# Rotations ahead of the value casts, and layer 0's last adds on VectorE with layer 1's tables and first weights in place early

## The chip, the cores and the metric

The kernel runs on one core of a Trainium2 chip. The metric is the device time of one execution in microseconds, median of three runs. The core has a matrix engine (TensorE, in the profile PE for its matmuls and PEld for the loading of stationary operands), a vector engine (VectorE, DVE), an activation engine (ScalarE, ACT), a general engine (GpSimd, POOL) and a queue from which most DMAs are issued (SyncE, SP). Each engine executes its instructions in the order in which they stand in its queue; between engines there are semaphores.

## The reference

A block of two layers for a diffusion model: 512 latent tokens and 256 context tokens, width 1024. Layer 0 has windowed attention with grouped keys and a sink, layer 1 differential attention with 8 heads. Each is followed by an MLP with squared ReLU. Cut to what matters:

```python
for i in range(DEPTH):                                # 2 layers
    mod_x = silu(c) @ w_ada[i] + b_ada[i]             # six vectors; mod_c likewise
    hx, hc = x * (1 + sc1) + sh1, ctx * (1 + csc1) + csh1
    ax, ac = mixer_i(hx, hc)                          # q, k rotated (x only), v not
    x  = layer_norm(alpha * x + g1 * ax)
    fx = square(relu((x * (1 + sc2) + sh2) @ w1)) @ w2
    x  = layer_norm(alpha * x + g2 * fx)              # ctx likewise in layer 0
```

In `mixer_i` the projections are `q = rope(hx @ wq)`, `k = rope(hx @ wk)`, `v = hx @ wv`. The rotation multiplies each half of a head by tables of cosines and sines. Everything is in 32 bits.

## The kernel before, in words

The 768 tokens are six blocks of 128 (`tb` 0 to 3 latent, 4 and 5 context). Every product is done three times at reduced width: an operand is split into a high part (a cast on ACT) and a low part (a subtraction on DVE), and `mm3` (L323 to L327) multiplies high by high, high by low and low by high into one PSUM bank. So each weight goes through `wsplit` (L300): a DMA into a raw buffer, ACT's cast `h`, DVE's subtraction `l`. The helper `split` does the same to activations.

The order of TensorE's instructions is written out by the kernel itself: `Flow` is a planner that runs jobs (Python generators) against estimated engine times and emits TensorE's work in the order in which its plan has the operands ready. Only TensorE's order is fixed in this way (`manual_schedule`); the order on DVE, ACT, POOL and SP is chosen by the framework when the kernel is built, within the data dependencies and the order of the program text, unless the kernel adds an order edge (`ORDER`). PSUM is divided into two double banks (`sS`, tiles of 1024) and four single banks (`sm_`, tiles of 512). A bank is given back by `give` when the planner sees its reader done; for the chip the wait is a semaphore.

Three places are touched.

*Start of layer 0.* `start_load` loads, for each quarter `g` of the width, two blocks of modulation weights, two slices of the tokens and one query weight `Wq[0]`. `start_x` modulates the tokens: for each slice ACT writes the high part, DVE the value and (for latent tokens) the low part, POOL the low part of the context tokens. `kv_job` and `proj` multiply. `kv_post` takes the keys and values of one block from PSUM: ACT copies the values to `vv`, DVE rotates the keys (three products, POOL adds them), and `split` makes the stacked operand that TensorE transposes into `kT`.

*End of layer 0.* `mlp_pipe` ends in `last_y`: the last products of the second MLP matrix. By then `fx` holds most of the MLP's output, and POOL folds it into `acc`, gated, in 24 operations (`fold`). The remaining products stay in PSUM. `final` multiplies each by the gate on DVE (`g_tmp`, in scratch buffers of tag `tmp`, of which there are three, shared with the normalised tiles `hx_v`) and adds the product to `acc`: on DVE where `last` is true, else on POOL. The statistics follow, then `normalise` and, in `ln_job`, transposes and the split operands `hx` of layer 1. In the second half (`half == 1`) only block 5 is added on DVE:

```python
r = gated_add(R.pool, lambda x: sm_.give(slot, x), acc[tb], half, pt, p, gates[0 if tb < NXB else 1],
              half == 1 if l else half == 0 or tb == ntb - 1)
```

*Start of layer 1.* `pre1` loads the weights of head 0 (four parts `u`) and multiplies blocks 0 to 3 while layer 0 ends. The rest happens once the pool of layer 0 is closed: the tables `cosT` and `sinT` are loaded, `proj1` multiplies blocks 4 and 5 and then the other heads, and `post1` takes each block from PSUM: first the values (`split` into `vt`), then the rotation of queries and keys, then `split` into `sk` and `sq`, which TensorE transposes to `kT_ps` and `qT_ps`. `scores1` needs all six blocks of a head.

## Time and profile before

| | |
|---|---|
| median of 3 runs | 1653.91 us (1649.16 to 1657.4) |
| profiled execution | 1652.57 us, of which the span from the first to the last instruction is 1650.8 |
| mean granted TensorE clock | 0.989 |
| TensorE busy | 1576.2 us (95%) |
| DVE / ACT / POOL busy | 1141.4 / 794.2 / 452.0 us |
| DMA | 181.18 MB, 110 GB/s on average |

Times in the profile are microseconds from the start of the span. A row of a timeline has the start, the duration, the engine, the line, the operation, out<-in, the shape and the count; in brackets stand the idle time of the engine just before it and what ended it. A row of waits has who waited for whom, the total, the number of times and the longest. Where a helper records an operation, the line is that of the helper (L260 DVE, L264 ACT, L268 POOL, L275 DMA, L314 the low part of a weight), and the tile names tell the place.

### The profile page before, as it was taken

The numbers are of one execution on the slowest core, as the hardware profiler recorded it, in microseconds if no ns is written. First come the engines' busy times: TensorE is split into PE (matmuls) and PEld (weight loads), VectorE is DVE, ScalarE is ACT, GpSimd is POOL, SyncE is SP. The second block draws the span as 40 slices with busy tenths as digits, with TensorE's granted clock in tenths as the row PEclk, the third lists the DMA queues.
The fourth block names the chain that finished last, engine by engine and source line by source line (L and its number), as shares of the span: only waits on it lengthen the run. The fifth ranks groups of instructions, "written<-read, shape, count | busy, mean of one in ns | idle before, by whom it ended". The sixth has DMA issues, their size and how long they took to land.

```text
span 1650.8 us, 25195 instructions
## 1 busy us (share of the span) xinstructions
PE 1576.2 (95%) x9465; PEld 1380.7 (84%) x9465; DVE 1141.4 (69%) x2201; ACT 794.2 (48%) x1683; POOL 452.0 (27%) x369
## 2 busy tenths in 40 slices
PE   7899999999999999999997999999989799999998
PEld 5788777789888888889986999899877788888896
DVE  4655676688786768877556777777665886565667
ACT  3465676375343343334416555555552745444550
POOL 1343544106111211221191222220100023233363
PEclk9999999999999999999998999999999999999999
DMA  9110550533344444444423122211122233333321
GB/s 373 43 52 20 192 179 27 187 132 123 101 156 156 146 131 130 163 130 153 153 68 115 49 74 64 75 46 39 49 95 110 93 118 109 103 102 102 99 74 59
DMA packets 66435, 181.18 MB, mean 110 GB/s; under 512 B 7368, under 2 KB 13320, under 8 KB 66312
## 3 DMA queue, kind: packets, MB, share of 16 engines
q1 hardware_dynamic: 66312, 179.56, 32.5%
q8 instruction: 74, 1.21, 0.3%
q14 instruction: 49, 0.40, 0.1%
HBM read 168.49 MB, written 11.04 MB: 109 GB/s over the span
## 4 chain that ended last, share of the span: by engine, by line
PE 69%; DVE 11%; ACT 6%; issue 5%; POOL 5%; DMA 4%; SPq 0%; DVEq 0%; POOLq 0%; ACTq 0%
PE y_ps L325 8%; PE y_ps L326 8%; PE y_ps L327 8%; PE h_ps L325 7%; PE h_ps L326 7%; PE h_ps L327 7%; PE qkv_ps L325 2%; PE qkv_ps L326 2%; PE qkv_ps L327 2%; PE o_ps L1379 2%; PE pT_ps L1397 2%; PE s_ps L1758 2%; POOL acc L268 1%; PE o_ps L1796 1%; DVE w_l L314 1%
## 5 line engine op out<-in xcount | busy, mean ns | idle before, releaser
L325 PE MATMUL y_ps<-w_h,hid 128*128 128x512 f32 (+1 forms) x648 | 255.4, 394 | 1.1 <-DVE fx L260 1.1
L326 PE MATMUL y_ps<-w_l,hid 128*128 128x512 f32 (+1 forms) x648 | 254.6, 393 | 0.9 <-DVE w_l L314 0.9
L327 PE MATMUL y_ps<-w_h,hid 128*128 128x512 f32 (+1 forms) x648 | 254.7, 393 | 0.0
L314 DVE TENSOR_TENSOR w_l<-w_raw,w_h 128x1024 fp32r<-128x1024 f32 (+1 forms) x133 | 160.8, 1219 | 58.9 <-ACT w_h L264 56.8
L264 ACT CAST w_h<-w_raw 128x1024 fp32r<-128x1024 f32 (+1 forms) x133 | 131.7, 1001 | 108.1 <-PE y_ps L327 76.4
L268 POOL TENSOR_TENSOR w_sum<-w_raw 128x512 f32<-128x512 f32 x26 | 59.1, 2274 | 329.0 <-DMA w_raw<-in_w 264.8
L260 DVE TENSOR_TENSOR w_half<-w_raw,w_half 128x512 fp32r<-128x512 f32 x130 | 107.8, 840 | 56.7 <-ACT w_half L264 56.2
L327 PEld LDWEIGHTS y_ps<-w_h,hid 128*128 128x128 f32 x648 | 122.0, 188 | 28.6
L326 PEld LDWEIGHTS y_ps<-w_l,hid 128*128 128x128 f32 x648 | 122.1, 188 | 26.4 <-DVE w_l L314 1.8
L325 PEld LDWEIGHTS y_ps<-w_h,hid 128*128 128x128 f32 x648 | 122.1, 188 | 25.9 <-DVE fx L260 1.5
L264 ACT CAST w_half<-w_raw 128x512 fp32r<-128x512 f32 x130 | 79.1, 621 | 131.8 <-PE h_ps L327 97.1
L325 PE MATMUL qkv_ps<-w_h,hx 128*128 128x384 f32 (+1 forms) x384 | 128.1, 334 | 3.0 <-ACT w_h L264 2.9
L326 PE MATMUL qkv_ps<-w_l,hx 128*128 128x384 f32 (+1 forms) x384 | 123.5, 322 | 1.7 <-DVE w_l L314 1.7
L327 PE MATMUL qkv_ps<-w_h,hx 128*128 128x384 f32 (+1 forms) x384 | 123.2, 321 | 0.0
L268 POOL TENSOR_TENSOR e<-e,sm 128x512 f32<-128x512 f32 (+2 forms) x96 | 92.7, 978 | 109.1 <-DVE sm L260 84.0
L264 ACT ACTIVATE relu<-relu 128x384 f32<-128x384 f32 (+3 forms) x104 | 69.3, 671 | 60.6 <-DVE relu L260 59.4
L260 DVE TENSOR_TENSOR fx<-y_ps,fx 128x512 f32<-128x512 f32 x110 | 75.2, 685 | 33.4 <-PE y_ps L327 33.0
L268 POOL TENSOR_TENSOR rope<-rope,rope 128x256 f32<-128x256 f32 (+1 forms) x40 | 33.9, 847 | 222.7 <-DVE rope L260 175.9
L268 POOL TENSOR_TENSOR w_raw<-w_raw,w_sum 128x512 f32<-128x512 f32 x26 | 39.2, 1508 | 178.3 <-DVE w_half L260 140.7
L673 DVE CUSTOM_DVE_ANT_0 w_raw<-w_raw,cB 128x512 f32<-128x512 f32 x112 | 84.1, 785 | 3.7 <-PE y_ps L327 3.2
L264 ACT ACTIVATE e<-e,nm 128x513 f32<-128x513 f32 (+2 forms) x96 | 65.9, 687 | 32.4 <-DVE nm L260 25.7
L325 PEld LDWEIGHTS qkv_ps<-w_h,hx 128*128 128x128 f32 x384 | 73.0, 190 | 4.8 <-ACT w_h L264 3.3
(268 smaller groups left out, 4323.9 us busy)
## 6 DMA issues: line engine op xcount, KB each, us to landing
w_raw<-in_w SPq DMA_DIRECT2D x128, 512.0 KB, 3.6
w_raw<-in_w_adaT SPq DMA_DIRECT2D x56, 512.0 KB, 3.8
w_raw<-in_w_ada SPq DMA_DIRECT2D x24, 512.0 KB, 3.8
w_raw<-in_b_w SPq DMA_DIRECT2D x32, 384.0 KB, 3.6
raw<-in_w_ada SPq DMA_DIRECT2D x16, 512.0 KB, 9.6
w_raw<-in_a_wq SPq DMA_DIRECT2D x8, 512.0 KB, 7.9
w_raw<-in_a_wo SPq DMA_DIRECT2D x8, 512.0 KB, 4.5
w_raw<-in_b_wo SPq DMA_DIRECT2D x8, 512.0 KB, 4.4
```

What stands on the lines that cost most here:

```text
L260: fn(**kw)
L264: fn(**kw)
L268: fn(**kw)
L314: last["split"] = nc.vector.tensor_tensor(**kw)
L325: nc.tensor.matmul(out=o, lhsT=lh, rhs=rh, start=start, stop=False, **kw)
L326: nc.tensor.matmul(out=o, lhsT=lh, rhs=rl, start=False, stop=False, **kw)
L327: last["pe"] = nc.tensor.matmul(out=o, lhsT=ll, rhs=rh, start=False, stop=stop, **kw)
L673: i = fn(**kw)
L1379: nc.tensor.matmul(out=po[odd * HD:odd * HD + HD, 0:256], lhsT=vv[:, kb, kvh], rhs=pt_[:, odd * 256:odd * 256 + 256], start=(i == 0), stop ...
L1397: nc.tensor.transpose(out=pp[:, c * P:(c + 1) * P], in_=es[j][:, i * P:(i + 1) * P], identity=ident)
L1758: nc.tensor.matmul(out=sp[:, c * 512:c * 512 + 384], lhsT=qTt[:, tt, hl, qb * P:(qb + 1) * P], rhs=kS[:, tt, c * 384:c * 384 + 384], start ...
L1796: nc.tensor.matmul(out=po[:, qp * 256:(qp + 1) * 256], lhsT=vt[:, kb, vl], rhs=pt_[:, pl, a * 256:a * 256 + 256], start=(kp == 0 and pl == ...
```

## The change

It has two parts. The first is in the order of the program text. In `kv_post` and `post1` the rotations, and for context blocks the key split, are stated ahead of the values' casts. In layer 0 the values of four blocks, and then of two, are copied by one instruction (`v_copy`). At the start of layer 0 the cast and the split of the last query weight get an order edge behind the last modulation of the tokens.

The second is at the border of the layers. All adds of `final` in layer 0 go to DVE. `fx` moves to a pool of its own on the right side of the memory, which is closed after the folds (`folded`), and a pool `early1` takes its place: it holds layer 1's tables, rotation scratch, `vt`, `sk`, `sq` and the residual tiles. In `pre1` the first two of head 0's four weights get buffers of their own (the MLP's `relu` and raw buffers), and all six blocks are multiplied there, the context blocks in single banks. The special latency that the planner assumed for the last block's normalisation (2.5) is dropped in favour of the common one (6.0).

```diff
@@ wsplit
-        a = ac(n, [q, hg], nc.scalar.copy, out=h[:, :n], in_=raw[:, :n])
+        last["cast"] = nc.scalar.copy(out=h[:, :n], in_=raw[:, :n])
+        a = fl.op("A", act(n), [q, hg])
@@ last_y, final
-                              half == 1 if l else half == 0 or tb == ntb - 1)
+                              half == 1 or l == 0)
...
                 for tb in range(ntb):
                     fold(half, tb, None)
+            R.folded()
@@ start_load
             Wq[0].append(wsplit(t["a_wq"][0, g]))
+            last["q"] = last["cast"], last["split"]
@@ start_x (ia: the last ACT modulation, id_: the last DVE low part)
+            if g == 3:
+                for w, x in zip(last["q"], (ia, id_)):
+                    tc.add_manual_dep(w.ins, x.ins.name, ORDER, reason="queue order")
@@ kv_post
+        def v_copy(tb, n, src, p):
+            return ac(n * P, [p], nc.scalar.copy, out=vv[:, tb:tb + n],
+                      in_=src.rearrange("p (b s g d) -> p b s g d", s=2, g=2, d=HD)[:, :, 1])
...
-            e = ac(P, [p], nc.scalar.copy, out=vv[:, tb], in_=vv_)
             if tb < NXB:
                 kr, e, r = rope(pool, kk_, tb, 2, p, ...)
                 if tb == NXB - 1:
-                    sS.give(kvslots[0], e)
+                    sS.give(kvslots[0], v_copy(0, NXB, kvS, e))
...
             if tb == NTB - 1:
-                sm_.give(kvslots[1], r)
+                sm_.give(kvslots[1], v_copy(NXB, NTB - NXB, kvm, r))
@@ layer 0's MLP
+    right = ExitStack()
+    fxpool = right.enter_context(tc.tile_pool(name="fx0", bufs=1, side="right", reuse_waits="tile"))
...
+            def folded(self):
+                right.close()
+                st2["ep"] = right.enter_context(tc.tile_pool(name="early1", bufs=1, side="right", reuse_waits="tile"))
...
-            fl.add(ln_job(pool, acc[tb], tb, st2["hx"], st2["A"], st2["B"], ready2, st, r, None,
-                          LNLAT if tb < NTB - 1 else 2.5), 0)
+            fl.add(ln_job(pool, acc[tb], tb, st2["hx"], st2["A"], st2["B"], ready2, st, r), 0)
@@ pre1
-            st2["W"] = [wsplit(t["b_w"][0, u], 768) for u in range(4)]
+            own = [pool.tile([P, n], F32R, name="w_" + x, tag=tag, bufs=2) for n, tag in ((TOK, "xr"), (1024, "raw"))
+                   for x in "hl"]
+            st2["W"] = W = [wsplit(t["b_w"][0, u], 768, hl=own[2 * u:2 * u + 2] + [None, None] if u < 2 else None)
+                            for u in range(4)]
...
+            for tb in range(NTB):
+                j = tb % 2
+                if tb >= NXB:
+                    yield sm_.ok
+                    pj, give = psm("qkv_ps"), (lambda x, i=sm_.take(): sm_.give(i, x))
+                else:
...
+                for u in range(4):
+                    yield W[u].t
+                    p = qkv_mm(W, st2["hx"], tb, pj, u)
+                    if tb == NTB - 1:
+                        fl.finish(W[u].rel)
+                st2["pre"][tb] = pj, p, give
@@ attn1 (cosT, sinT, rope, vt, sk, sq, rs_* now from ep = st2["ep"])
-        lamv = pool.tile([P, 4, HD], F32, name="lamv", tag="rope", bufs=2)
+        lamv = pool.tile([P, 4, HD], F32, name="lamv", tag="oraw", bufs=3)
@@ post1
-            _, e = split(P, p, pt[:, 256:384], vt[:, tb, 0], vt[:, tb, 1])
             if isx:
-                qk, e2, r = rope(pool, pt[:, 0:256].rearrange("p (g d) -> p g d", d=HD), tb, 4, p)
+                qk, e2, r = rope(ep, pt[:, 0:256].rearrange("p (g d) -> p g d", d=HD), tb, 4, p)
                 kr = qk[:, 2:4]
-                give([e, e2])
...
+            def v_split(d):
+                return split(P, d, pt[:, 256:384], vt[:, tb, 0], vt[:, tb, 1])[1]
+            if isx:
+                give(v_split(e2))
...
-                give([e, d1])
+                give(v_split(d1))
```

## The prediction

> **What bounds the kernel now.** The page comes first: which engine fills the span, and what clock it was granted.

> ```profile
> span 1650.8 us, 25195 instructions
> PE 1576.2 (95%) x9465; PEld 1380.7 (84%) x9465; DVE 1141.4 (69%) x2201; ACT 794.2 (48%) x1683; POOL 452.0 (27%) x369
> PEclk9999999999999999999998999999999999999999
> ```

> TensorE is busy for 1576.2 of 1650.8 us, and neither its 9465 matmuls nor their shapes are touched by the change. So the change can win only from the 74.6 us in which TensorE stands still, and from stretches at a lower granted clock (the 8 in PEclk, 22nd of the 40 slices, 867 to 908 us, is one). Those 74.6 us come next, from the view of TensorE's own waits; its columns are total us, times, longest. These are the rows that the edits can reach.

> ```profile
> PE kT_ps L1662 <- DVE sk L260: 7.8, 6, 2.3
> PE xn_t L550 <- DVE g_tmp L584: 5.4, 3, 2.8
> PE qkv_ps L325 <- ACT w_h L264: 2.9, 1, 2.9
> PE xn_t L550 <- POOL rstd L268: 1.8, 1, 1.8
> PE qkv_ps L326 <- DVE w_l L314: 1.7, 2, 1.2
> PE q_ps L325 <- DVE rope L260: 1.5, 1, 1.5
> PE xn_t L550 <- ACT hx_v L264: 0.9, 1, 0.9
> PE kv_ps L327 <- POOL hx L268: 0.7, 1, 0.7
> ```

> Then I place them with the view of stages: start and end, width, busy PE, PEld, DVE, ACT, POOL, then the granted clock.

> ```profile
> 50.00:66.00 16.00, 13.83 (x85) 11.81 (x83) 11.65 (x31) 7.42 (x19) 5.78 (x7) 1.00 0.13 37
> 848.00:863.00 15.00, 15.00 (x66) 12.06 (x65) 6.75 (x7) 1.06 (x1) 15.00 (x11) 1.00 0.18 54
> 863.00:892.50 29.50, 18.59 (x98) 14.22 (x96) 21.30 (x44) 17.19 (x50) 8.87 (x11) 0.95 0.18 71
> 888.50:900.00 11.50, 7.06 (x26) 6.28 (x27) 9.02 (x18) 10.68 (x28) 0.55 (x1) 0.55 0.32 103
> 1168.00:1180.00 12.00, 9.68 (x40) 8.01 (x39) 8.55 (x13) 5.44 (x12) 0.00 (x0) 0.72 0.47 164
> ```

> Three places matter. The key and value stage of layer 0 loses 16.00 - 13.83 = 2.2 us. The seam between the layers loses 29.50 - 18.59 = 10.9 us up to 892.5 and 1.2 more behind it (the longest wait for w_l): 12.1, the sum of the xn_t rows (5.4 + 1.8 + 0.9) and of w_h 2.9 and w_l 1.2, but for rounding. There the clock falls too: a mean of 0.55 over 11.5 us is (1 - 0.55) / 0.5 x 11.5 = 10.3 us at half speed, if half is the low state. TensorE worked 7.06 / 11.5 of the time, so 6.3 us at half speed, of which half, 3.2 us, is lost. Layer 1 loses 7.8 us in front of the key transposes, and a second dip, 0.72 over 12 us, follows the longest of these waits (2.3). In between, as in 848 to 863, TensorE is full: what is gained in these places stays gained.

> **The change, part by part.** *Start of layer 0.* The cast and the split of the last query weight now go behind the last tokens' modulation.

> ```profile
> 52.27 1.04 ACT L264 CAST w_h<-w_raw 128x1024 fp32r<-128x1024 f32 x1
> 53.65 1.22 DVE L314 TENSOR_TENSOR w_l<-w_raw,w_h 128x1024 fp32r<-128x1024 f32 x1
> 58.83 0.29 DVE L260 TENSOR_TENSOR kr<-kv_ps,c_cosT 128x128 f32<-128x128 f32 x1 [1.22 <-ACT v L264]
> 59.84 0.29 DVE L260 TENSOR_TENSOR kr<-kv_ps,c_cosT 128x128 f32<-128x128 f32 x1 [0.46 <-ACT v L264]
> ```

> They stood in front of it for 1.04 us on ACT and 1.22 on DVE; the 0.7 us wait of kv_ps for the modulated tokens (through POOL) is shorter than both, so it goes: **-0.7**. Late next is that weight's low half, some 2 us later than 54.9 (53.65 + 1.22). The key and value products of the last tokens, which wait for the same modulation and come first on TensorE, hide it: nothing; without that cover up to 2 us. The rotations now precede the value copies: the two rows show DVE held by ACT's copy v. The second hold is 0.46 us, and of the first, 1.22, one copy can go, 0.27 by the value cast of the same width at 906.11 below (the rest is the wait for the product): 0.7 us earlier on DVE, which is what the 1.5 us wait of q_ps for a rotation hangs on: **-0.7**. Six value copies become two wider ones on ACT, which is busy 7.42 of 16 us: nothing.

> *The seam: adds.* Five of the six second-half adds of layer 0 leave POOL.

> ```profile
> 863.41 0.69 DVE L260 BATCH_NORM_STATS2 bn<-acc 128x6 f32<-128x512 f32 x1 [8.63 <-POOL acc L268]
> L260 DVE TENSOR_TENSOR acc<-acc,g_tmp x7: 691/983/1779, 834.8 to 888.8; 128x512 f32<-128x512 f32 x7
> L268 POOL TENSOR_TENSOR acc<-acc,g_tmp x5: 1273/1289/1332, 862.1 to 880.2; 128x512 f32<-128x512 f32 x5
> ```

> POOL was full to 863 with the folds (15.00 of 15.00), so the first add started at 862.1, and DVE sat idle 8.63 us for it. Meanwhile the three scratch buffers were held by products waiting to be added, no further product could be drained, and the transposes waited for PSUM: that is how I read the 5.4 us of xn_t on g_tmp. Removed: 5 x 1.29 us of POOL and ten crossings. Added: five adds on DVE, each 0.69 (alone) to 1.78 us (beside POOL): 3.5 to 8.9. I take about 4.5, since only the first one or two can meet folds. DVE had 29.5 - 21.3 = 8.2 us idle in the seam, and 8.25 (15.00 - 6.75) before it, so even 8.9 fits; were that idle gone, it would be added to the path. Each block's power for 1/std stays on POOL behind the folds, so the normalising can't start much before 863 and the first transposes gain little: the 1.8 on rstd stays, and so does the 0.9 on ACT. Gone: **-5.4**. The last block's longer planning delay (6.0 in place of 2.5) lets the planner put layer 1 products ahead of its transposes: no instruction, no price of its own.

> [...]

> *The seam: weights.* Two of layer 1's first four weights get buffers of their own, in place of the slots that layer 0's last weights hold.

> ```profile
> 846.64 1.06 ACT L264 CAST w_h<-w_raw 128x1024 fp32r<-128x1024 f32 x1 [18.13 <-PE y_ps L327]
> 891.47 2.41 ACT L264 CAST w_h<-w_raw 128x768 fp32r<-128x768 f32 x3
> 900.01 0.34 PE L327 MATMUL qkv_ps<-w_h,hx 128*128 128x384 f32 x1
> 905.73 0.34 PE L327 MATMUL qkv_ps<-w_h,hx 128*128 128x384 f32 x1
> 922.78 0.27 ACT L264 CAST sk<-qkv_ps 128x128 fp32r<-128x128 f32 x1
> 925.40 0.27 ACT L264 CAST sk<-qkv_ps 128x128 fp32r<-128x128 f32 x1
> ```

> Their casts ran at 891.47, right where TensorE waited 2.9 and 1.2 us. ACT stood idle for 18.13 us before 846.64: the two go there, and the other two find slots that are released one product earlier. Same four loads, same casts. Gone: **-2.9 and -1.2**. With the waits the dip goes: **-3.2**. What remains of the waits, 2.7, is spread over several places.

> *The seam: six blocks ahead.* All six first products of layer 1 now come before any of its transposes; the second row lies 33 matmuls behind the first, so a block of 24 takes 24 x (905.73 - 900.01) / 33 = 4.2 us. Then come the transposes and scores of head 0, for which the rotations and casts of all six blocks must be done. No row shows that wait. Bounds: 0, if the posts run beside the blocks, and 21.4, if all of them run with TensorE empty (the stretch in the slower rival below). The two context blocks come last and their key casts are 925.40 - 922.78 = 2.6 us apart; one such step I leave uncovered: **+2.6**, nearer the lower end since the posts of four blocks can run under the later blocks.

> *Tables.* Cosine, sine and rotation scratch now lie where fx was, free from the end of the folds at 862. Same loads, same SP queue. They are not on the path before (the slower rival has the row): 0.

> *Layer 1, eight heads.* Nothing is added or removed; the value cast and split go behind the rotation or, in context blocks, behind the key split.

> ```profile
> 1217.41 0.28 DVE L260 TENSOR_TENSOR vt<-qkv_ps,vt 128x128 fp32r<-128x128 f32 x1
> 1217.61 1.22 DVE L314 TENSOR_TENSOR w_l<-w_raw,w_h 128x1024 fp32r<-128x1024 f32 x1
> 1217.72 0.27 ACT L264 CAST sk<-qkv_ps 128x128 fp32r<-128x128 f32 x1 [0.37 <-DVE vt L260]
> 1219.17 0.34 PE L1662 MATMUL kT_ps<-identr,sk 128*128 128x128 f32 x2 [1.41 <-DVE sk L260]
> 1171.51 0.36 PE L1662 MATMUL kT_ps<-identr,sk 128*128 128x128 f32 x2 [2.32 <-DVE sk L260]
> 1032.57 1.57 DVE L260 SCALAR_TENSOR_TENSOR e<-e,nl,e 128x768 f32<-128x768 f32 x1
> 1034.48 0.34 PE L1662 MATMUL kT_ps<-identr,sk 128*128 128x128 f32 x2 [1.72 <-DVE sk L260]
> 1210.42 0.34 PE L1662 MATMUL kT_ps<-identr,sk 128*128 128x128 f32 x2 [1.44 <-DVE sk L260]
> ```

> At 1217.72 ACT's key cast waited 0.37 us for DVE's value split; both read the same PSUM tile. With the keys first, cast and split come 0.6 us sooner, and DVE's weight split (1.22) no longer slips in between: 1.3 of the 1.41. At 1171.51 0.6 of 2.32. At 1210.42 the keys come through a rotation, whose start moves up by one cast and one split: between 0 and 1.44, and I take the middle, 0.7. At 1034.48 the wait is for DVE's 1.57 us behind something else: 0. The other two (7.8 - 6.9 = 0.9 together) are left as they are. **-2.6**, bounds 0 and -5.2 (the last three stalls whole). The price on the other side: a PSUM slot is given back later by one cast and one split, less the rotation they had delayed, some 0.2 us; no quoted row has TensorE wait for such a slot here.

> Sum: -0.7 - 0.7 - 5.4 - 4.1 - 3.2 + 2.6 - 2.6 = **-14.1 us**. The profiled execution took 1652.6 us (span 1650.8 and 1.8 around it): 1638.5. It lies 1.3 under the median of 1653.9, so against the median **1640**.

> **The rivals.** *All stalls go*: the remaining 2.7, the 2.6, another 0.8 at the start (2.2 - 1.4), 2.6 more in layer 1 and its dip, which by the same working (0.28 / 0.5 x 12 = 6.7 us, 9.68 / 12 of it worked, half lost) costs 2.7: 11.4 more, 1629. For it: TensorE has four blocks of 4.2 us and two smaller ones ready. Against: the stalls have several causes. *The rotations change nothing* (DVE and ACT order themselves by what is ready): 3.3 less, 1643. *The scratch buffers still bind*: products and normalised tiles share three of them, so 5.4 and the dip stay: 8.6 less, 1648, no measurable change. For it: the wait names g_tmp, not the add. Against: DVE frees a buffer in 0.69 us without a crossing.

> *Slower: layer 1 starts late.* The place is the first rotation of head 0.

> ```profile
> 899.70 0.38 SPq L283 DMA_DIRECT2D c_cosT<-in_cosT  x1
> 906.11 0.27 ACT L264 CAST vt<-qkv_ps 128x128 fp32r<-128x128 f32 x1 [2.52 <-PE qkv_ps L327]
> 927.16 0.37 ACT L264 CAST kS<-kT_ps 128x256 fp32r<-128x256 f32 x1 [1.21 <-PE kT_ps L1662]
> ```

> The tables stood in SP's queue until 899.70, behind weight loads that wait for buffers; everything on DVE queues behind a rotation without its table. Before, the posts of six blocks took from 906.11 to 927.5: 21.4 us, under which TensorE had products. These now run earlier. If the tables land only as the sixth block ends, TensorE empties for up to 21.4 us and the clock dips (3.2): 24.6 in place of my 2.6, 1662. It decides once that gap passes 13.5 us (14.1 + 2.6 - 3.2). Against: the tables were asked for 6 us before their use, and their memory is free sooner.

> [...]

> **How the numbers follow.** Forecast 0.45; all gone 0.12; rotations nothing 0.13; buffers bind 0.20; late start 0.10. A change under 0.5%, 8.3 us, can't be told from none here: faster means under 1645.6, slower over 1662.2. The first three cases give 0.70, of which I move 0.02 over the bound: faster 0.68. The late start falls on both sides of its bound, and re-planning may shift TensorE's order anywhere: slower 0.07, same 0.25. The forecast's own range is 1633 to 1646; for 8 in 10 it reaches from near the case of no stalls to most of the late start: 1627 to 1658.

> **What would show it.** Right: no POOL add on acc from g_tmp after the folds; DVE idle before 863 filled; under 5 us of TensorE idle between 863 and the sixth block; granted clock 1.00 there; casts of two b_w weights before 860; key waits of 5 us or less in layer 1. Wrong: xn_t still waiting on g_tmp, a TensorE gap over 5 us before head 0's scores, or a new dip there.

## The result, and the profile after

| | before | changed |
|---|---|---|
| median | 1655.91 us (7 runs) | 1665.06 us (7 runs, 1660.79 to 1669.03) |
| ratio to before | | 1.0062, interval 1.0047 to 1.0078 |
| profiled execution: span | 1650.8 us | 1663.3 us |

The change made the kernel 0.62% slower, some 10 us, where 14 us less were forecast. The page of the changed kernel, cut to three lines that answer to the first three of the prediction:

```profile
span 1663.3 us, 25213 instructions
PE 1581.6 (95%) x9465; PEld 1384.3 (83%) x9465; DVE 1148.9 (69%) x2206; ACT 795.1 (48%) x1679; POOL 432.0 (26%) x364
PEclk9999999999999999999999999999999999999999
```

The same matmuls take 5.4 us more (1581.6 - 1576.2), and TensorE stands still for 7.1 us more (81.7 in place of 74.6). To see where, I laid the two executions side by side by TensorE's own milestones, the first or last start of a product as the trace's groups give it:

| stretch, up to | before, us | changed, against before |
|---|---|---|
| last key and value product of layer 0 | 58.9 | -1.8 |
| last attention product of layer 0 | 245.7 | +2.6 |
| last product of layer 0's output projection | 41.9 | 0.0 |
| last product of hx0m with a whole weight (start of layer 0's MLP) | 58.5 | +3.9 |
| last MLP product of layer 0 | 420.2 | -1.0 |
| first product of layer 1 (the seam) | 67.3 | -7.6 |
| first scores of layer 1 | 34.5 | +3.0 |
| last attention product of layer 1 | 318.6 | +5.9 |
| last product of layer 1's output projection | 37.3 | +7.0 |
| end | 367.9 | +0.5 |

The seam did become shorter: 7.6 us up to layer 1's first product, of which 3.0 are given back before its first scores. The loss lies in places that the prediction priced at nothing or as a gain. These are single profiles; below, a stage of a profile is shown to move by some 4 us without any edit to it. The view of TensorE's waits over the whole changed kernel names the places (total, times, longest; y_ps holds the products of the second MLP matrix or of the output projection, s_ps the scores, e their exponentials, pT the transposed probabilities, o_ps the attention output):

```profile
PE kT_ps L1692 <- DVE sk L260: 9.2, 7, 2.2
PE s_ps L1788 <- ACT e L264: 6.2, 6, 1.4
PE y_ps L326 <- ACT w_h L309: 4.7, 2, 4.2
PE y_ps L326 <- DVE g_tmp L585: 3.3, 3, 2.0
PE o_ps L1826 <- DVE pT L260: 2.7, 5, 0.6
PE q_ps L326 <- DVE rope L260: 1.2, 1, 1.2
```

The seam's rows of before are gone: no xn_t on g_tmp or rstd, no qkv_ps on w_h. In their place stand y_ps on g_tmp, scores on ACT's exponentials, more waits for the split keys, and one of 4.2 us for a weight. The view of stages shows the same (start and end, width, busy PE, PEld, DVE, ACT, POOL, then the granted clock):

```profile
856.00:860.00 4.00, 3.13 (x13) 1.95 (x12) 4.00 (x4) 0.00 (x0) 4.00 (x2) 1.00 0.00 0
860.00:888.60 28.60, 26.60 (x132) 21.70 (x131) 22.93 (x46) 14.47 (x41) 10.01 (x11) 1.00 0.40 140
908.00:912.00 4.00, 4.00 (x36) 4.00 (x35) 0.00 (x0) 0.00 (x0) 0.00 (x0) 1.00 0.03 6
912.00:926.00 14.00, 10.77 (x72) 9.44 (x72) 9.06 (x29) 9.66 (x28) 2.20 (x3) 1.00 0.17 56
926.00:1250.60 324.60, 304.08 (x2031) 286.03 (x2030) 224.65 (x463) 175.37 (x399) 59.23 (x69) 0.97 0.16 52
1264.00:1296.00 32.00, 27.31 (x110) 21.24 (x109) 19.20 (x34) 5.44 (x6) 1.43 (x3) 0.89 0.54 197
```

TensorE idles 2.0 of 28.6 us in the seam, and the clock there is whole. Over the eight heads (926 to 1250.6) the clock is 0.97 where it was 0.99: three dips of 6.8 us in place of one. In the output projection, which was full before (37.40 of 37.40 us at a clock of 1.00), TensorE idles 4.7 us at a clock of 0.89.

### The profile page after: what moved, and what is told of

It reads as the page before. It is cut to its first block, busy times and chain, and to the rows that moved or that the text cites. A ratio compares the mean times of both kernels' runs of the same rounds, so it can differ in the third digit from the quotient of the medians.

```text
span 1663.3 us, 25213 instructions
## 1 busy us (share of the span) xinstructions
PE 1581.6 (95%) x9465; PEld 1384.3 (83%) x9465; DVE 1148.9 (69%) x2206; ACT 795.1 (48%) x1679; POOL 432.0 (26%) x364
## 3 DMA queue, kind: packets, MB, share of 16 engines
q8 instruction: 74, 1.21, 0.3%
## 4 chain that ended last, share of the span: by engine, by line
PE 72%; DVE 12%; ACT 6%; DMA 4%; POOL 3%; issue 3%; SPq 0%; DVEq 0%; ACTq 0%; POOLq 0%
PE y_ps L327 9%; PE y_ps L326 8%; PE y_ps L328 8%; PE h_ps L326 6%; PE h_ps L328 6%; PE h_ps L327 6%; PE qkv_ps L326 2%; PE o_ps L1391 2%; PE qkv_ps L328 2%; PE qkv_ps L327 2%; PE pT_ps L1409 2%; PE s_ps L1788 2%; PE o_ps L1826 2%; ACT e L264 2%; DVE w_l L315 1%
## 5 line engine op out<-in xcount | busy, mean ns | idle before, releaser
L326 PE MATMUL y_ps<-w_h,hid 128*128 128x512 f32 (+1 forms) x648 | 255.7, 395 | 4.8 <-DVE g_tmp L585 3.3
L327 PE MATMUL y_ps<-w_l,hid 128*128 128x512 f32 (+1 forms) x648 | 254.9, 393 | 2.2 <-DVE w_l L315 2.2
L326 PEld LDWEIGHTS y_ps<-w_h,hid 128*128 128x128 f32 x648 | 122.1, 188 | 31.1 <-DVE g_tmp L585 4.4
L260 DVE TENSOR_TENSOR w_half<-w_raw,w_half 128x512 fp32r<-128x512 f32 x130 | 107.9, 841 | 55.7 <-ACT w_half L264 55.2
L327 PEld LDWEIGHTS y_ps<-w_l,hid 128*128 128x128 f32 x648 | 122.1, 188 | 28.2 <-DVE w_l L315 3.8
L264 ACT CAST w_half<-w_raw 128x512 fp32r<-128x512 f32 x130 | 79.1, 621 | 130.4 <-PE h_ps L328 95.5
L326 PE MATMUL qkv_ps<-w_h,hx 128*128 128x384 f32 (+1 forms) x384 | 128.4, 334 | 1.1 <-DVE vt L260 0.9
L268 POOL TENSOR_TENSOR w_sum<-w_raw 128x512 f32<-128x512 f32 x26 | 42.6, 1637 | 328.7 <-DMA w_raw<-in_w 191.0
L327 PE MATMUL qkv_ps<-w_l,hx 128*128 128x384 f32 (+1 forms) x384 | 123.1, 321 | 0.3 <-DVE w_l L315 0.3
L268 POOL TENSOR_TENSOR e<-e,sm 128x512 f32<-128x512 f32 (+2 forms) x96 | 93.8, 993 | 100.8 <-DVE sm L260 64.3
L264 ACT ACTIVATE relu<-relu 128x384 f32<-128x384 f32 (+3 forms) x104 | 69.3, 671 | 62.8 <-DVE relu L260 61.5
L260 DVE TENSOR_TENSOR fx<-y_ps,fx 128x512 f32<-128x512 f32 x110 | 75.2, 686 | 33.7 <-PE y_ps L328 33.4
L268 POOL TENSOR_TENSOR rope<-rope,rope 128x256 f32<-128x256 f32 (+1 forms) x40 | 34.6, 865 | 241.5 <-DVE rope L260 158.3
L268 POOL TENSOR_TENSOR w_raw<-w_raw,w_sum 128x512 f32<-128x512 f32 x26 | 39.2, 1506 | 198.2 <-DVE w_half L260 161.3
L264 ACT ACTIVATE e<-e,nm 128x513 f32<-128x513 f32 (+2 forms) x96 | 65.9, 688 | 34.5 <-DVE nm L260 26.8
L264 ACT ACTIVATE e<-s_ps,nm 128x768 f32<-128x768 f32 x64 | 57.5, 901 | 44.7 <-DVE nm L260 43.6
```

Of the source, the lines that this page charges most:

```text
L260: fn(**kw)
L264: fn(**kw)
L268: fn(**kw)
L326: nc.tensor.matmul(out=o, lhsT=lh, rhs=rh, start=start, stop=False, **kw)
L327: nc.tensor.matmul(out=o, lhsT=lh, rhs=rl, start=False, stop=False, **kw)
```

## The experiments

Each ratio is to the kernel before, from runs on the same chip, with its 95% interval. One per cent is 16.5 us.

### The three parts by themselves

*Layer 0's rotations and query weight alone:*

```diff
+        last["cast"] = nc.scalar.copy(out=h[:, :n], in_=raw[:, :n])
+            last["q"] = last["cast"], last["split"]
+                    tc.add_manual_dep(w.ins, x.ins.name, ORDER, reason="queue order")
-            e = ac(P, [p], nc.scalar.copy, out=vv[:, tb], in_=vv_)
+                    sS.give(kvslots[0], v_copy(0, NXB, kvS, e))
```

> Layer 0's rotations and the last query weight's place alone; seam and layer 1 as before. Theory (the time was lost at places that the diff doesn't name): the last key and value product comes about 1.8 us earlier (57.1 in place of 58.9), this is given back by the end of layer 0's attention, and the total stays within 2 us of the kernel before. Rival (a gain in a full stretch stays, as the prediction had it): 1.4 us earlier from there to the end. Second rival: the 4.0 us lost at the start of layer 0's MLP (347 to 410 us) come from this part's new order on TensorE; then this kernel is 3 to 4 us slower than before.

*Layer 1's reordering alone:*

```diff
-            _, e = split(P, p, pt[:, 256:384], vt[:, tb, 0], vt[:, tb, 1])
...
-                give([e, e2])
+            if isx:
+                give(v_split(e2))
...
-                give([e, d1])
+                give(v_split(d1))
```

> Layer 1's order of rotation, key split and value split alone; everything up to the first products of layer 1 is as before. Theory (this part costs what the eight heads lost, 892 to 1246 us: about 5.6 us of waits and 3 us of lower clock): 6 to 9 us slower than before, the key transposes waiting for VectorE (kT_ps<-DVE sk) 7 us or more in all, and a granted clock of about 0.97 over the heads. Rival (the prediction): 2.6 us faster, key waits 5 us or less. Second rival (the heads' loss comes from the seam's six blocks): no change beyond 1 us.

*The seam alone: everything else of the change.*

```diff
-                              half == 1 if l else half == 0 or tb == ntb - 1)
+                              half == 1 or l == 0)
+            R.folded()
-        lamv = pool.tile([P, 4, HD], F32, name="lamv", tag="rope", bufs=2)
+        lamv = pool.tile([P, 4, HD], F32, name="lamv", tag="oraw", bufs=3)
...
```

> The seam alone (adds on VectorE, weights, six blocks, tables and scratch where fx was); both rotations as before. Theory: seam 7 to 8 us shorter up to layer 1's first product; 4 us lost at 347 to 410 us; 7 us lost in layer 1's output projection, where the last b_wo load stands behind the loads of acc, which lie on buffers that the last heads still use; the eight heads as before: 2 to 4 us slower than before in all. Rival (the heads' loss belongs to the seam part): 8 to 12 us slower. Second rival (the 4 us belong to the start of layer 0): about the time of before.

| part | ratio | us |
|---|---|---|
| layer 0's rotations | 1.0006 (0.9989 to 1.0022) | +1.0 |
| layer 1's reordering | 1.0039 (1.0019 to 1.0059) | +6.5 |
| seam | 1.0020 (0.9999 to 1.0040) | +3.3 |
| sum | | +10.8 |
| the change | 1.0062 (1.0047 to 1.0078) | +10.3 |

The parts add up within their intervals, and each time lies where its main theory had it. Where layer 0's part gains or loses the profiles don't tell: it ends its first stretch at 57.7 and the attention behind it at 304.4, but the ten profiles without it end them anywhere from 57.4 to 59.2 and from 302.9 to 305.2. Layer 1's part lengthens the eight heads by 7.6 us in its profile, and its waits there are those of the changed kernel (kT_ps on sk 6.9, scores on e 6.3, o_ps on pT 2.6). The seam part loses 6.5 us in the output projection and leaves the heads alone (-1.2).

One figure of my theory fell: the 3.9 us at the start of layer 0's MLP belong to no part. Layer 1's part has the same order of instructions up to layer 1, and yet its profile shows 3.6 of them there, while layer 0's part shows none. The last section comes back to this.

### The output projection: what lies where

In the changed kernel the last weight of the output projection arrives too late. Its issue on SP, its cast on ACT, and the end of the last heads' split outputs on DVE:

```profile
1266.07 1.75 SPq L275 DMA_DIRECT2D acc<-x_res  x4
1268.60 0.46 SPq L275 DMA_DIRECT2D w_raw<-in_b_wo  x1
1277.44 1.04 ACT L309 CAST w_h<-w_raw 128x1024 fp32r<-128x1024 f32 x1 [11.52 <-DMA w_raw<-in_b_wo]
1278.54 0.80 PE L326 MATMUL y_ps<-w_h,oT 128*128 128x512 f32 x1 [4.23 <-ACT w_h L309]
1265.29 1.35 DVE L260 TENSOR_TENSOR oT<-oraw,oT 128x512 fp32r<-128x512 f32 x2
```

The same two issues in the kernel before:

```profile
1222.53 12.23 SPq L275 DMA_DIRECT2D acc<-x_res  x4
1253.03 0.33 SPq L275 DMA_DIRECT2D w_raw<-in_b_wo  x1
```

The weight stands behind the four loads of acc in SP's queue. These used to start at 1222 and now start at 1266.07, while the last uses of oraw run (from 1265.29). The reason that I proposed: with the rotation scratch gone from the pool `attn1` and the lambda vector's tiles on the tag oraw, oraw is allocated first in that pool, and layer 1's acc, first in the next one, lies on it. To test it, the same kernel with those two tiles on another tag, so that the keys' buffers come first:

```diff
-        lamv = pool.tile([P, 4, HD], F32, name="lamv", tag="oraw", bufs=3)
+        lamv = pool.tile([P, 4, HD], F32, name="lamv", tag="kS1", bufs=2)
-        lamp = pool.tile([P, 2, HD], F32, name="lamp", tag="oraw", bufs=3)
+        lamp = pool.tile([P, 2, HD], F32, name="lamp", tag="kS1", bufs=2)
```

> The changed kernel, but with the lambda vector's two small tiles on the keys' tag (kS1) in place of the raw attention outputs' (oraw), so that kS1 and not oraw comes first in the pool, and layer 1's residual lands on it later. Nothing of the arithmetic changes. Theory: acc<-x_res is issued before 1250 us in place of 1266, the last b_wo load is in front of its cast when that is reached, the wait of 4.2 us at 1278.54 and the clock dip behind it go: 7 us faster than the changed kernel, about 1658. Rival (the load is late for another reason, or another wait takes its place): no more than 1 us.

Measured: 1.0019 (1.0004 to 1.0035), 7 us faster than the changed kernel (1.0062, 1.0047 to 1.0078). The output projection is back at its length of before (24.0 us from the norm's last product to its own last, +0.0), with these issues on SP:

```profile
1228.14 11.48 SPq L275 DMA_DIRECT2D acc<-x_res  x4
1256.39 0.33 SPq L275 DMA_DIRECT2D w_raw<-in_b_wo  x1
```

The seam part repeats it: +3.3 us above, and -3.0 with the tiles moved (below). So 7 of the 10 us hung on two tag names, and showed some 360 us after the tiles with these tags were used.

### Inside the seam

The seam with the tiles moved in this way is the base for two more, each with one piece taken back:

```diff
# adds back on POOL
-                              half == 1 or l == 0)
+                              half == 1 if l else half == 0 or tb == ntb - 1)
# four blocks ahead in place of six
-            for tb in range(NTB):
+            for i in range(2):
```

> The seam part alone (no reordered rotation) with the lambda tiles on the keys' tag. TensorE's and VectorE's orders are those of the seam part alone; only addresses differ. Theory: the 6.5 us lost in layer 1's output projection by the seam part alone are gone, so about 3 us faster than before (1651), with two added waits for g_tmp (3 us) in the seam and one of 2 to 3 us in front of the first key transposes. Rival (the six blocks and the full VectorE eat the whole gain): 0 to 1 us faster than before.

> As the run beside it, but with four of layer 1's first products ahead of the transposes, as before the change, in place of six. Theory (the single scratch buffers of the split keys and queries let no block be posted until TensorE has transposed the one before, so six blocks ahead only leave TensorE empty behind them): the wait of 2 to 3 us in front of the first key transposes goes or shrinks below 1 us, and the stretch from layer 1's first product to its first scores is 3 to 5 us shorter than with six blocks. Rival (the posts take that long anyway): the same stretch, within 1 us.

> As the first run of these, but the five second-half adds of layer 0 back on POOL, with the planner's delay of before. Theory (the adds on VectorE remove the 5.4 us of xn_t on g_tmp, but cost two waits of about 1 to 2 us because they collide with POOL's folds): the waits of xn_t for g_tmp come back (4 to 6 us) and those of y_ps for g_tmp go; 1 to 3 us slower than with the adds on VectorE. Rival (the adds give nothing net): the same time within 1 us or faster.

| kernel | ratio | us |
|---|---|---|
| seam, tiles moved | 0.9982 (0.9968 to 0.9997) | -3.0 |
| the same, adds on POOL | 1.0015 (0.9998 to 1.0033) | +2.5 |
| the same, four blocks ahead | 0.9970 (0.9957 to 0.9982) | -5.0 |

The adds on VectorE are worth 5.5 us, more than that run's theory had and as much as the prediction said; the two intervals only just fail to meet. TensorE's waits from 825 to 930 us (the larger rows), first with the adds on POOL, then with them on VectorE:

```profile
PE xn_t L550 <- DVE g_tmp L584: 5.2, 3, 2.8
PE y_ps L325 <- DVE g_tmp L584: 1.4, 2, 1.1
PE xn_t L550 <- DVE acc L535: 1.3, 1, 1.3
PE y_ps L326 <- DVE w_l L314: 0.8, 2, 0.6
```

```profile
PE y_ps L325 <- DVE g_tmp L584: 3.5, 3, 2.0
PE kT_ps L1678 <- DVE nlam L1641: 2.6, 1, 2.6
PE y_ps L326 <- DVE w_l L314: 0.9, 2, 0.6
```

The waits of xn_t go (5.2 and 1.3, and 0.9 for hx_v). Of the waits of y_ps for g_tmp, 1.4 stand there with the adds on POOL too, and so does nearly all of that for w_l; what the adds on VectorE bring is one new wait of 2.0. So 7.4 us of waits went and some 2 came.

The run with the adds on POOL also shows what the rest of the seam is worth without them: weights, clock and six blocks, forecast at -4.1 - 3.2 + 2.6 = -4.7, came to +2.5 (-0.3 to +5.5). Its waits for the weights w_h are gone, but the first keys (2.6) and g_tmp (1.4) stand in their place, and the clock over 825 to 930 us is 0.95, as before the change.

With four blocks the wait for the first keys (2.6) is gone, but others stand in its place (qkv_ps on kS 2.2, s_ps on kS 1.6), and the stretch to the first scores is 1.6 us shorter, not 3 to 5. The two times are 2 us apart with intervals that overlap, so whether four blocks are better is not shown. Nor do six blocks alone make that stretch longer: with four it takes 38.0 us, where the kernel before, also with four, takes 34.5.

### Layer 1's reordering taken apart

```diff
# context blocks only: blocks with a rotation as before
+                e = split(P, p, pt[:, 256:384], vt[:, tb, 0], vt[:, tb, 1])[1]
                 qk, e2, r = rope(...)
-                give(v_split(e2))
+                give([e, e2])
# rotated blocks only: context blocks as before
+            else:
+                e = v_split(p)
```

> Of layer 1's reordering only the context blocks' half: the value split behind the key split; blocks with a rotation as before. Theory (the loss comes from the rotated blocks, whose value split now stands behind three more operations and gives its PSUM slot back later): about the time of before, or up to 2 us faster, key waits 5 us or less. Rival (the loss comes from the context blocks: the key split slips behind the next head's weight splits and the norm's split): 4 to 7 us slower than before, with three key waits of 1.8 us behind the norm's transposes.

> Of layer 1's reordering only the rotated blocks' half: the value split behind the rotation; context blocks as before. The whole reordering gave +6.5 us against the kernel before and the context half alone -4.3. Theory (the two halves add): 8 to 12 us slower than before, waits of scores for ACT's exponentials and of o_ps for pT as with the whole reordering. Rival (the loss lies in the two together): within 3 us of the kernel before.

The context half: 0.9974 (0.9958 to 0.9990), 4.3 us faster. The rotated half: 1.0049 (1.0030 to 1.0068), 8.1 us slower. So one edit held a gain and a loss that is larger. Together they make +3.8 where the whole gave +6.5, which the intervals allow. Over the heads the key waits are 7.1 us before, 4.0 with the context half and 10.0 with the rotated half; the waits of scores for exponentials (1.5 before) are 3.9 and 4.9. The context half's own profile is not shorter over the heads (318.0 us in place of 318.6), so its gain rests on the repeated runs.

Why the rotated half costs, there were two theories: the planner, told of a later bank, orders TensorE's work otherwise; or the new order on ACT and VectorE costs by itself. The next kernel accounts the value split to the planner as before, so that TensorE's order is row for row that of the kernel before, and only issues it later:

```diff
+                e = fl.op("D", dve(P), [fl.op("A", act(P), [p])])
                 qk, e2, r = rope(...)
-                give(v_split(e2))
+                nc.scalar.copy(out=vt[:, tb, 0], in_=pt[:, 256:384])
+                nc.vector.tensor_tensor(out=vt[:, tb, 1], in0=pt[:, 256:384], in1=f(vt[:, tb, 0]), op=ALU.subtract)
+                give([e, e2])
```

> The rotated blocks' value cast and split issued behind the rotation as in the run beside it, but accounted to the planner in the order of before, so that TensorE's order of work is exactly that of the kernel before. Theory (the loss comes from the TensorE order that the planner chooses when it sees a value split and its PSUM slot come later, not from VectorE's and ACT's own order): the loss of the run beside it is gone; within 2.5 us of the kernel before. Rival (the later value split and PSUM slot cost on the chip): as slow as the run beside it. The prediction's step: 2 us or more faster than before.

Measured: 1.0043 (1.0026 to 1.0059), 7.1 us slower. My theory fell; the order on the two engines costs by itself. With TensorE's order equal the traces can be laid on each other. The kernel before, around two places:

```profile
940.02 0.59 ACT L264 CAST pT<-pT_ps 128x512 fp32r<-128x512 f32 x1 [1.79 <-PE pT_ps L1824]
941.06 0.30 ACT L264 CAST sk<-rope 128x128 fp32r<-128x128 f32 x1 [0.45 <-POOL rope L268]
970.92 0.86 PE L1758 MATMUL s_ps<-kS,qT 128*128 128x384 f32 x4
972.22 0.95 DVE L260 TENSOR_REDUCE nm<-s_ps 128x1 f32<-128x768 f32 x1
973.09 1.01 DVE L260 SCALAR_TENSOR_TENSOR e<-e,nl,e 128x768 f32<-128x768 f32 x1
974.01 0.28 DVE L260 TENSOR_TENSOR sk<-rope,sk 128x128 fp32r<-128x128 f32 x1
```

And this kernel:

```profile
939.76 0.27 ACT L1649 CAST vt<-qkv_ps 128x128 fp32r<-128x128 f32 x1 [1.21 <-DVE rope L260]
941.13 0.30 ACT L264 CAST sk<-rope 128x128 fp32r<-128x128 f32 x1 [1.10 <-POOL rope L268]
942.53 1.06 ACT L264 CAST pT<-pT_ps 128x512 fp32r<-128x512 f32 x2
945.52 1.65 PE L1804 MATMUL o_ps<-pT,vt 128*128 128x256 f32 x6 [2.59 <-DVE pT L260]
975.51 0.86 PE L1766 MATMUL s_ps<-kS,qT 128*128 128x384 f32 x4
976.84 1.00 DVE L260 SCALAR_TENSOR_TENSOR e<-e,nl,e 128x768 f32<-128x768 f32 x1
977.77 0.28 DVE L260 TENSOR_TENSOR sk<-rope,sk 128x128 fp32r<-128x128 f32 x1
978.31 1.81 DVE L260 TENSOR_REDUCE nm<-s_ps 128x1 f32<-128x768 f32 x2
980.33 0.97 PE L1766 MATMUL s_ps<-kS,qT 128*128 128x384 f32 x4 [1.14 <-ACT e L264]
```

At the first place ACT's value cast now waits 1.21 us for VectorE's rotation, and the key split's cast behind it 1.10 us for POOL's part of the rotation. Before, the cast of the transposed probabilities stood in front of that key cast (940.02 and 941.06); here it stands behind it (942.53 and 941.13), 2.5 us later, and TensorE waits 2.59 us for pT. At the second, the earlier rotation brings the combining of two exponentials and the key split ahead of the scores' maximum on VectorE. That maximum started 1.30 us after its scores (972.22 - 970.92) and now starts 2.80 after them (978.31 - 975.51). The exponentials follow it on ACT, they release the scores' bank, and the next scores wait 1.14 us. Over all eight heads the waits of scores for exponentials grow from 1.5 to 5.0 us and those of o_ps for pT from nothing to 4.9, while the key waits shrink from 7.1 to 5.7: 7.0 us together, as much as the kernel lost.

### What helps, in one kernel

The seam with four blocks ahead and the tiles moved, and the value split behind the key split in context blocks only; the second kernel adds layer 0's part of the change:

```diff
+                              half == 1 or l == 0)
+        lamv = pool.tile([P, 4, HD], F32, name="lamv", tag="kS1", bufs=2)
+                e = split(P, p, pt[:, 256:384], vt[:, tb, 0], vt[:, tb, 1])[1]
-                give([e, d1])
+                give(v_split(d1))
...
```

> What the runs so far show to help, in one kernel: the seam part with four blocks ahead and the lambda tiles on the keys' tag (-5.0 us alone), and layer 1's value split behind the key split in context blocks only (-4.3 alone). Theory (the parts add): 8 to 10 us faster than before, about 1645. Rival (a new order eats one of them): 3 to 6 us faster.

> The same kernel with layer 0's rotations and the last query weight's place as in the change (+1.0 us alone, not told apart from none). Theory: the 1 to 2 us gained at the start are given back within layer 0's attention; within 2 us of the run beside it. Rival (the start's gain is kept once the rest is full): 1.5 to 3 us faster than it.

Measured: 0.9934 (0.9913 to 0.9956), median 1644.93, and with layer 0's part 0.9924 (0.9905 to 0.9942), median 1642.05. Both beat the kernel before and the changed one; against the kernel before they gain 10.9 and 12.6 us. The sum of the parts was -9.3. Whether layer 0's part helps the two runs don't tell.

## Why the prediction was wrong, step by step

*Start of layer 0, -0.7 - 0.7.* The kv_ps wait for POOL is gone, as forecast; the q_ps wait fell from 1.5 to 1.2 only, so 0.3 of the second 0.7. The -1.8 at the last key and value product proves neither, since that product moves by as much between profiles without the edit. In time the part is worth +1.0 (-1.8 to +3.6), which holds nothing as well as the -1.4. One premise did fail: that in between TensorE is full, so that what is gained stays gained. It was backed by 848 to 863 alone. The stretch behind the start isn't full; in the changed kernel it is

```profile
60.00:305.50 245.50, 237.05 (x1705) 185.49 (x1703) 157.99 (x445) 147.95 (x415) 104.34 (x105) 0.99 0.24 81
```

with 8.4 us idle (7.8 before), in which a gain can be lost; whether it was lost there is not shown.

*Adds, -5.4.* Right in size: 5.5 us between the two kernels that differ in it, and the waits that it names go. That the number fits so well is partly luck: waits of xn_t for rstd (1.8) and hx_v (0.9) went too, which the prediction had left standing, and one wait of 2.0 us for g_tmp came, behind VectorE's work on the next blocks. The cost on VectorE was read rightly. The first and the second of the five moved adds in the changed kernel:

```profile
862.13 1.53 DVE L260 TENSOR_TENSOR acc<-acc,g_tmp 128x512 f32<-128x512 f32 x1
869.29 0.69 DVE L260 TENSOR_TENSOR acc<-acc,g_tmp 128x512 f32<-128x512 f32 x1
```

The other three took 0.69 each, so the five took 4.3 us where the prediction had 4.5: only the first met a fold. The upper bound of 8.9, all five at 1.78, was not met. Longer adds are seen beside the folds, where VectorE and POOL are both full (4.00 of 4 us each from 856 to 860, above): there the six first-half adds, which were on VectorE before as well, took 0.97 to 1.77.

*Weights, -2.9 - 1.2, and the clock, -3.2.* Right in the changed kernel: the two casts run at

```profile
838.37 0.84 ACT L309 CAST w_h<-w_raw 128x768 fp32r<-128x768 f32 x1 [6.20 <-DVE g_tmp L585]
843.24 0.84 ACT L309 CAST w_h<-w_raw 128x768 fp32r<-128x768 f32 x1 [4.03 <-DMA w_raw<-in_b_w]
```

the waits are gone, and the clock is 1.00 up to 926. That the clock stays up was partly luck: with the tiles moved, the same change shows a clock of 0.86 over 912 to 924, behind the wait for the first keys. And the waits that went did not shorten the kernel by their sum: with the adds on POOL, the weights, the clock and the six blocks came to +2.5 in place of -4.7.

*Six blocks ahead, +2.6.* The place was right: TensorE waits 2.20 us for the first key split behind the sixth block, and 3.2 us idle lie between 912 and 926. The reason that I see is not a lack of time but of buffers. From 908 to 912 VectorE and ACT do nothing at all (0.00 of 4.00 each, above), with products of earlier blocks waiting. Their split keys have one buffer, and TensorE empties it only behind the sixth block. I had argued that posts run under later blocks. Then the weights of the next head come in between, since the sixth block's last product frees their slots as well:

```profile
912.24 1.57 ACT L309 CAST w_h<-w_raw 128x768 fp32r<-128x768 f32 x2 [5.49 <-PE qkv_ps L328]
914.19 0.95 DVE L315 TENSOR_TENSOR w_l<-w_raw,w_h 128x768 fp32r<-128x768 f32 x1
915.25 0.28 DVE L260 TENSOR_TENSOR sk<-rope,sk 128x128 fp32r<-128x128 f32 x1
```

The key cast on ACT (914.47) stands behind the two weight casts and the key split on VectorE behind the weight split, so the 2.20 us need not be the buffer's alone. This reading is argued from the trace; neither a second buffer nor later weights were tried. In the seam alone the stretch grew by 5.

*Tables, 0.* They were asked for at 852.76 in place of 899.70, and nothing waited. The slower rival's 1662 lies near the measured 1665 by luck: the gap that it named did not come. But the step looked only at what the moved tiles bring early. It didn't ask what comes to lie where they had been: there the change lost 7 us, as much as in any other place, and no step of the prediction touches it.

*Layer 1, eight heads, -2.6.* Wrong in sign: +6.5. The step priced earlier keys and a bank given back 0.2 us later. It didn't price the wait that the edit adds, the value cast on ACT for a rotation on VectorE, and didn't name what is queued behind it; nor did it see that an earlier rotation puts the key split in front of the scores' maximum. TensorE waited for keys at six places, but between them it lived on scores. For context blocks, where there is no rotation to wait for, the sign was right: 1.3 + 0.6 there, measured 4.3 (1.7 to 6.9).

So the sum fails in this way: -1.4 became +1.0, not told apart from -1.4 or from nothing; the seam's -10.1 (-5.4 - 4.1 - 3.2 + 2.6) became -3.0 with the tiles moved, and the part of it that failed is that of weights, clock and six blocks; the heads' -2.6 became +6.5; and a term of +7 was missing. Of the signs that I had named for a right prediction all but the last were seen (key waits of 9.2 in place of 5), and none of those named for a wrong one. They all lay in the seam, and the loss lay elsewhere.

## What to carry to other kernels

A tile that moves to another pool changes which tile comes first in the pool that it leaves, and so who must be done before the next stage's loads can start (7 us here): after such a move, compare when every later load is issued. Stating an operation earlier is a loan from whatever stood in front of it on the same engine (7.1 us slower here, with TensorE's order equal); before moving one, ask which instruction of that queue TensorE's banks hang on. An edit to several kinds of blocks should be timed for each kind by itself: here one half was worth -4.3 us and the other +8.1.

## What the runs showed of the hardware

*One instruction, two durations.* The same sum on POOL, in kernels with the same order of work up to there, took 21.01 us or 4.57. Its row in the profiles of the kernel before, and of layer 1's part alone:

```profile
378.44 21.01 POOL L268 TENSOR_TENSOR w_sum<-w_raw 128x512 f32<-128x512 f32 x1 [23.59 <-DVE acc L260]
```

```profile
378.24 4.57 POOL L268 TENSOR_TENSOR w_sum<-w_raw 128x512 f32<-128x512 f32 x1 [23.62 <-DVE acc L260]
```

Of the fourteen profiles seven have each. With 4.57 the stretch of layer 0's first MLP products took 61.2 to 63.3 us, with 21.01 it took 58.5 to 60.4: the shorter sum goes with the longer stretch. Between those two profiles, eight VectorE operations on fx take 0.68 us in the mean and then 0.82, and TensorE is busy 38.0 and then 36.0 us of the 38 from 373 to 411; the changed kernel, whose sum took 4.57 at 380.24, has 0.82 and 35.8. This is the 3.9 us of the first table, and it isn't the change's. That the sum takes either time with the same order of work is shown by these rows alone: each kernel was profiled once, but five of them have the same order of work on every engine up to there, and three of the five show 21 us and two 4.57. What decides between the two is not shown.

*The same wait, with and without a clock dip.* In the changed kernel two equal waits for split keys, each with the stage around it:

```profile
1006.42 0.34 PE L1692 MATMUL kT_ps<-identr,sk 128*128 128x128 f32 x2 [1.77 <-DVE sk L260]
1181.44 0.34 PE L1692 MATMUL kT_ps<-identr,sk 128*128 128x128 f32 x2 [1.77 <-DVE sk L260]
```

```profile
1003.00:1015.00 12.00, 10.23 (x44) 8.60 (x43) 8.88 (x13) 5.84 (x12) 0.11 (x1) 0.72 0.45 146
1178.00:1190.00 12.00, 10.23 (x62) 9.17 (x61) 10.07 (x18) 7.12 (x15) 0.37 (x2) 1.00 0.48 165
```
